# The last product of a decoder block: a gate applied in PSUM, stores queued behind all loads, more rooms, one root for four tiles

## The chip, the cores and the metric

One core of a Trainium2 chip runs the whole kernel. The metric is device time in microseconds (us) of one execution; the number given for a kernel is the median of its runs. Engines: TensorE (PE) multiplies, VectorE (DVE), ScalarE (ACT) and GpSimd (POOL) work on elements, SyncE (SP) issues the DMAs. Each engine serves its instructions in the order in which they stand in its own queue.

## What is computed

The reference is one hybrid decoder block on 1024 tokens of width 1024: sparse attention heads and Mamba-2 heads from one input projection, merged by gates, an output projection, then a SwiGLU feed-forward part and a last norm. Only its end matters here:

```python
h = rms_norm(x, norm2_w[l]) * (1.0 + sc2) + sh2
x = x + gt2 * ((jax.nn.silu(h @ w_gate[l]) * (h @ w_up[l])) @ w_down[l])
return rms_norm(x, norm_f_w)      # x * rsqrt(mean(x^2) + 1e-6) * norm_f_w
```

All is float32. The feed-forward width is 2816, 22 blocks of 128.

## The kernel before

Every float32 product is made of three products of a split operand: a high part (ACT copies it, rounded, into the type float32r) and a low part (DVE or POOL subtracts the high part from the source); `mm3k` (lines 292 to 297) issues high times high, high times low, low times high. The pair of high and low part of a 128x512 block is called a piece.

The down projection (`down`, from line 1975) is a Strassen-Winograd product: seven products instead of eight, in the order P1, P2, P6, P7, P5, P4, P3 (`DOWN`). Each has 11 blocks b of the inner dimension (NB) and four token tiles j, so 44 jobs of three matmuls 128x128x512; the four tiles of a product accumulate in four PSUM banks. For each block two pieces are needed, one of activations (from `actd` in DRAM) and one of `w_down` or of sums of its blocks (`wsd`). `down_load` (line 1938) loads each into a row, a 128x512 staging buffer out of 18 (`row`, lines 1479 to 1489), and lets `part` (line 1712) split it into a room: there are 12 rooms for pieces (`piece`, lines 1491 to 1503), six blocks. For one of the two pieces of a block the low part is made on DVE, for the other on POOL. The loads are asked for six blocks ahead of the block that PE is at (line 2053). For P3 the piece of `w_down` is first multiplied on POOL with gate 2, which lies in `acc[:, 9]` (line 1956).

What a product gives is used in `ends` (from line 1998). After P2, P5 and P4 a half (512 columns) of a tile of the residual x2 is completed: a sum with the bank, a multiplication with gate 2 (`times`, line 1996), the addition to x2 (line 1993); after P3 its bank is only added to x2 (line 2015), because the gate is in the weights already. When a half is complete, `square` (line 2065) lets ACT sum its squares. P2 completes the left halves of the even tiles (t = 0, 2, 4, 6), P5 the right halves of the odd ones, P4 the left halves of the odd ones, P3 the right halves of the even ones. When both halves of a tile are there, `final` (line 2077) takes a root for it (`rsqrt`, lines 249 to 274: three scalings and shifts for the first guess, then three steps of two instructions each) and scales the two halves with the root and the final gain `nf`, and a store of each half to `out` is put into SP's queue (line 2092). For the left halves of the even tiles POOL multiplies with `nf` beforehand (`self.pre`, line 2038) and ACT scales; all others are scaled by DVE in one instruction (L2089).

In P3 the last four blocks are done tile by tile (`LAST = 4`): blocks 0 to 6 for all four tiles, then blocks 7 to 10 for tile j = 0, then for j = 1, and so on. The even tile t is 2j.

The order in each queue is fixed while the program is built, by a small planner (`Flow`, lines 105 to 211). Each step has an engine (A, V, G, D stand for ACT, DVE, POOL and SP's DMAs), a cost in us and a list of what it needs; the planner plays the engines forward with these costs and writes an instruction into its engine's queue when, by that clock, it can start; `first=True` puts a step ahead of the others that are waiting. The chip then runs the queues in that order, at its own speed. DVE's 128x512 operation is planned at 0.6 us times a reserve of 1.15.

Of the kernel before, what the change touches and what calls it, by code (L numbers as in the profile page):

```python
# [11 lines left out]
I32 = mybir.dt.int32  # L12
# [200 lines left out]

class Weights:
# [25 lines left out]
class Kern:  # L240
# [8 lines left out]
    def rsqrt(self, needs, r, n, c, eps, slow=1.0):  # L249
# [16 lines left out]
        e = V(0.07 * slow, needs, lambda: E.tensor_scalar(col(0), col(0), c * 2.0 ** 26, eps * 2.0 ** 26, op0=OP.mult, op1=OP.add))  # L266
        e = V(0.07 * slow, [e], lambda: E.tensor_single_scalar(col(2).bitcast(I32), col(0).bitcast(I32), 1, op=OP.arith_shift_right))

        e = V(0.07 * slow, [e], lambda: E.tensor_scalar(col(2).bitcast(I32), col(2).bitcast(I32), -1, 0x5F3759DF - 2 ** 31,
                                                 op0=OP.mult, op1=OP.add))  # L270
        for f in (3.0, 12.0, 768.0):
            e = V(0.19 * n * slow, [e], products)
            e = V(0.07 * n * slow, [e], lambda f=f: step(f))
# [1217 lines left out]
    def piece(self):  # L1491

        b = Buf(self.rings["pc"], None)

        def make():
            if b.i < 8:
                r, = self.room(self.xroom[b.i])
                return r[:, 0:512], r[:, 512:1024]
            m = b.i - 8
            return tuple(w.t.rearrange("p k c -> p (k c)")[:, 512 * m:512 * m + 512] for w in self.room(*self.wroom))  # L1500

        b.make = make
        return b
# [434 lines left out]
    def down_load(self, p, b):  # L1938
# [5 lines left out]
        for n in range(2):  # L1944
# [9 lines left out]
            if p == 3 and n:  # L1954

                d = G(1.23, [d, self.g2op], lambda x=x: nc.gpsimd.tensor_tensor(x.t, x.t, self.acc[:, 9], op=OP.mult))
# [18 lines left out]
    def down(self):  # L1975
# [14 lines left out]
        LAST = 4  # L1990
# [7 lines left out]
        def ends(p, j, ps, op):  # L1998
# [14 lines left out]
            if p == 3:  # L2013
                t, cs = 2 * j, slice(512, 1024)
                e = V(0.6, [op, ua[j]], lambda: nc.vector.tensor_tensor(x2[:, t, cs], x2[:, t, cs], ps.t, op=OP.add), first=True)
                ps.until(e)
                self.square(t, 1, e)
                self.final(t, nf, nfop)
                return
# [16 lines left out]
            if p == 2:  # L2036

                self.pre[t] = G(1.23, [self.sq[t][0], nfop], lambda: nc.gpsimd.tensor_tensor(xs(), xs(), nf(cs), op=OP.mult))
            if p == 4:
                self.final(t, nf, nfop)  # L2040

        for n, p in enumerate(self.DOWN):
# [3 lines left out]
            for b, j in jobs:  # L2046
# [4 lines left out]
                if j == 0:  # L2051
                    i = n * NB + b
                    while len(self.dl) < min(i + 6, 7 * NB):
                        self.down_more()
                (xp, xe), (wp, we) = self.dl[p, b]
# [9 lines left out]
    def square(self, t, cb, need):  # L2065
# [3 lines left out]
        if t not in self.rf:  # L2069
            self.rf[t] = self.buf("rq" if t % 2 else "rf", [128, 6], f"rq_nf{t}")  # L2070
            self.sq[t] = {}
        r = self.rf[t]
        self.sq[t][cb] = e = A(0.62, [need, jk, r], lambda: nc.scalar.activation(
            jk.t, self.x2[:, t, cs], AF.Square, accum_out=r[:, cb:cb + 1]))
        jk.until(e)

    def final(self, t, nf, nfop):
        nc, x2, sq, r = self.nc, self.x2, self.sq[t], self.rf[t]
# [3 lines left out]
        ends = []  # L2082
        for cb in range(2):
            cs = slice(512 * cb, 512 * cb + 512)
            x = lambda cs=cs: x2[:, t, cs]
            if cb == 0 and t in self.pre:
                w = A(0.61, [self.pre[t], e], lambda x=x: nc.scalar.activation(x(), x(), AF.Copy, scale=r[:, 2:3]))
            else:
                w = V(0.6, [e, nfop], lambda x=x, cs=cs: nc.vector.scalar_tensor_tensor(  # L2089
                    x(), x(), r[:, 2:3], nf(cs), op0=OP.mult, op1=OP.mult))  # L2090
            ends.append(w)
            D(0.73, [w], lambda x=x, cs=cs: nc.sync.dma_start(self.out[t * 128:(t + 1) * 128, cs], x()))
        r.until(*ends)
# [340 lines left out]
```

## Time and profile before

| | us |
|---|---|
| median of 3 runs | 2545.92 (2544.04 to 2547.81) |
| the profiled execution | 2542.33 |
| its span, first to last instruction | 2540.50 |
| PE busy | 2439.7, 96% |
| DVE busy | 1803.7, 71% |
| ACT busy | 1238.7 |
| POOL busy | 1169.3 |
| mean granted clock of TensorE | 0.988 |

The span is what the profiler saw between the first and the last instruction; the execution's own time has 1.83 us more. The page also lists the chain that ended last, waits between engines and the order of time; times in the trace count from the span's start. The down projection begins at 2302.15.

### The profile page before, as it was taken

The numbers are of one execution on the slowest core, as the hardware profiler recorded it, in microseconds if no ns is written. First come the engines' busy times: TensorE is split into PE (matmuls) and PEld (weight loads), VectorE is DVE, ScalarE is ACT, GpSimd is POOL, SyncE is SP. The second block draws the span as 40 slices with busy tenths as digits, with TensorE's granted clock in tenths as the row PEclk, the third lists the DMA queues.
The fourth block names the chain that finished last, engine by engine and source line by source line (L and its number), as shares of the span: only waits on it lengthen the run. The fifth ranks groups of instructions, "written<-read, shape, count | busy, mean of one in ns | idle before, by whom it ended". The sixth has DMA issues, their size and how long they took to land. (4 is left out here: it accounts for less than half of the span.)

```text
span 2540.5 us, 39589 instructions
## 1 busy us (share of the span) xinstructions
PE 2439.7 (96%) x13674; PEld 2082.0 (82%) x13674; DVE 1803.7 (71%) x3937; ACT 1238.7 (49%) x2640; POOL 1169.3 (46%) x931
## 2 busy tenths in 40 slices
PE   5999999999999999999999899999989999999996
PEld 5999878889889888988877677878978888888885
DVE  7644787876766687765467786778787676664769
ACT  4421667666656566655555455532452332324443
POOL 2112474735465646464533341201355565555655
PEclk8999999999999999999999899999999999999998
DMA  7433443323335423233355675427323232337753
GB/s 249 131 124 98 141 120 92 108 80 100 92 100 173 141 95 114 80 101 97 122 173 184 224 234 186 157 65 253 125 72 112 91 112 93 103 121 283 226 159 112
DMA packets 265161, 345.55 MB, mean 136 GB/s; under 512 B 21112, under 2 KB 177528, under 8 KB 264448
## 3 DMA queue, kind: packets, MB, share of 16 engines
q1 hardware_dynamic: 264960, 343.02, 42.1%
q8 instruction: 108, 1.77, 0.3%
q14 instruction: 93, 0.76, 0.1%
HBM read 247.13 MB, written 95.81 MB: 135 GB/s over the span
## 5 line engine op out<-in xcount | busy, mean ns | idle before, releaser
L2190 POOL TENSOR_SCALAR P<-P,sm,gate 128x640 f32<-128x640 f32 (+7 forms) x256 | 215.2, 851 | 247.1 <-DVE sm L2187 186.6
L2261 DVE TENSOR_TENSOR kv<-tp,kv 128x512 fp32r<-128x512 f32 (+1 forms) x296 | 189.8, 657 | 108.1 <-ACT kv L2260 106.9
L2260 ACT ACTIVATE kv<-tp 128x512 fp32r<-128x512 f32 (+1 forms) x296 | 165.1, 574 | 184.0 <-PE tp L2257 176.6
L2181 ACT ACTIVATE P<-P,sm 128x640 f32<-128x640 f32 (+7 forms) x256 | 187.5, 734 | 45.9 <-DVE sm L2177 43.7
L1070 PE MATMUL o<-kv 128*128 128x512 f32 x528 | 189.6, 411 | 12.4 <-DVE kv L2261 8.8
L2172 PE MATMUL S<-kv,Q 128*128 128x384 f32 (+5 forms) x768 | 182.6, 336 | 3.0 <-DVE sm L2177 3.0
L2177 DVE CUSTOM_DVE_ANT_0 P<-S,kb 128x256 f32<-128x256 f32 (+5 forms) x256 | 120.5, 495 | 56.7 <-PE tp L2257 29.5
L1137 DVE SCALAR_TENSOR_TENSOR u<-xr,hcw,u 128x512 f32<-128x512 f32 x144 | 150.2, 1043 | 13.3 <-ACT u L1140 8.3
L295 PE MATMUL fps<-hT_hi,whi_x 128*128 128x512 f32 x384 | 157.3, 410 | 0.1
L1717 ACT ACTIVATE x1r<-ex 128x512 fp32r<-128x512 f32 x147 | 89.7, 627 | 135.4 <-POOL ex L1736 31.2
L1851 DVE TENSOR_TENSOR ex<-ex,gu 128x512 f32<-128x512 f32 x122 | 82.1, 684 | 99.1 <-PE gu L297 98.1
L2257 PE MATMUL tp<-id,P 128*128 128x128 f32 x1056 | 151.8, 272 | 0.5 <-POOL P L2190 0.5
L297 PE MATMUL fps<-hT_hi,wlo_x 128*128 128x512 f32 x384 | 151.0, 393 | 0.0
L296 PE MATMUL fps<-hT_lo,whi_x 128*128 128x512 f32 x384 | 151.0, 393 | 0.0
L295 PE MATMUL fps<-whi_z,hT_hi 128*128 128x256 f32 x512 | 149.8, 293 | 0.1
L1719 DVE TENSOR_TENSOR x1r<-ex,x1r 128x512 fp32r<-128x512 f32 x102 | 122.6, 1213 | 33.3 <-ACT x1r L1717 33.0
L2257 PEld LDWEIGHTS tp<-id,P 128*128 128x128 f32 x1056 | 127.2, 140 | 21.1 <-POOL P L2190 0.8
L297 PE MATMUL fps<-whi_z,hT_lo 128*128 128x256 f32 x512 | 144.4, 282 | 0.0
L296 PE MATMUL fps<-wlo_z,hT_hi 128*128 128x256 f32 x512 | 144.3, 282 | 0.0
L2172 PEld LDWEIGHTS S<-kv,Q 128*128 128x128 f32 x768 | 128.2, 189 | 17.9 <-DVE sm L2177 2.4
L1070 PEld LDWEIGHTS o<-kv 128*128 128x128 f32 x528 | 95.7, 189 | 34.6 <-DVE kv L2261 16.7
L2331 POOL TENSOR_TENSOR dx<-xs,hd 128x512 f32<-128x512 f32 x32 | 43.4, 1355 | 170.2 <-DVE yy L2373 127.9
(443 smaller groups left out, 8022.3 us busy)
## 6 DMA issues: line engine op xcount, KB each, us to landing
wada<-w_ada SPq DMA_DIRECT2D x40, 512.0 KB, 4.2
ex<-actd SPq DMA_DIRECT2D x73, 256.0 KB, 3.1
actd<-ex SPq DMA_DIRECT2D x69, 256.0 KB, 2.0
ac<-acd SPq DMA_DIRECT2D x32, 512.0 KB, 5.0
raw_x<-w_in SPq DMA_DIRECT2D x24, 512.0 KB, 4.4
ws<-w_down SPq DMA_DIRECT2D x44, 256.0 KB, 3.6
wsd<-ws SPq DMA_DIRECT2D x88, 128.0 KB, 1.8
ff<-w_gate SPq DMA_DIRECT2D x22, 512.0 KB, 5.0
```

The lines of the kernel that those rows point to most:

```text
L295: mm(ps, lh, rh, start=k == 0, stop=False)
L296: mm(ps, lh, rl, start=False, stop=False)
L297: mm(ps, ll, rh, start=False, stop=k == kt - 1)
L1070: nc.tensor.matmul(o.t.rearrange("p h q -> p (h q)"), vst(), pair()[m], start=n + m == 0, stop=n == u.total - 1 and m == 1)
L1137: nc.vector.scalar_tensor_tensor(u.t, xr[:, k:k + N2], hcw[:, ft, k:k + 1], u.t, op0=OP.mult, op1=OP.add)
L1719: return E(cost, [x], lambda: eng.tensor_tensor(k4(p.t[1]), src(), k4(p.t[0]), op=OP.subtract), first=first)
L2172: mm(sp[:, :w], q, kvb.kv[:, br, r, first + c0:first + c1], start=r == 0, stop=r == 1)
L2181: ex = A(0.26 + 0.8333e-3 * n, [mx], lambda: nc.scalar.activation(P[:, :n], P[:, :n], AF.Exp, bias=sm[:, 1, h:h + 1], scale=-1.0, accum_ou ...
L2190: nc.gpsimd.tensor_scalar(P[:, :n], P[:, :n], sm[:, 3, m:m + 1], k.gate[:, i, self.h0 + m, br + 1:br + 2], op0=OP.mult, op1=OP.mult)
L2257: nc.tensor.transpose(tp[:, h * 128:h * 128 + 128], P, k.id)
L2260: hi = A(0.064 + 0.104 * n, [op, pair], lambda: nc.scalar.activation(pair()[0][:, c], tp[:, c], AF.Copy))
L2261: lo = V(0.068 + 0.133 * n, [hi], lambda: nc.vector.tensor_sub(pair()[1][:, c], tp[:, c], pair()[0][:, c]))
```

## The change

- Gate 2 is no longer multiplied into the pieces of `w_down` for P3 on POOL. Instead, each bank of P3 is multiplied with it in PSUM on DVE, ahead of the addition to x2.
- P3's last six blocks, not four, are done tile by tile.
- There are 20 rooms for pieces: eight more in M1, the low parts of the feed-forward's input, free after the last gate/up product. The loads are asked for nine blocks ahead, not six.
- The four odd tiles get one root together after P4. Their sums of squares lie in `acc[:, 12]`; the root works on 128x4 operands, so a step is three instructions (two multiplications for the products, one for the step) for all four tiles. Even tiles keep a root each.
- The right halves of the odd tiles, completed by P5, are multiplied with `nf` on POOL beforehand and scaled on ACT; their left halves are scaled by DVE.
- The stores of the odd tiles are queued after the last load has been asked for, and need it (`self.dlast`). The stores of the even tiles are queued as before.

```diff
+class Roots:
+    def __getitem__(self, key):
+        return self.buf[:, 12, key[1]]
...
+        if n > 2:
+            def products():
+                y, t = col(n), col(2 * n)
+                E.tensor_tensor(t, y, y, op=OP.mult)
+                E.tensor_tensor(t, t, col(0), op=OP.mult)
+            def step(f):
+                y, t = col(n), col(2 * n)
+                E.scalar_tensor_tensor(y, t, -f, y, op0=OP.add, op1=OP.mult)
...
+            if b.i > 11:
+                return tuple(self.M1[:, (b.i - 12) // 2, 2 * ((b.i - 12) % 2) + r] for r in range(2))
...
-            if p == 3 and n:
-                d = G(1.23, [d, self.g2op], lambda x=x: nc.gpsimd.tensor_tensor(x.t, x.t, self.acc[:, 9], op=OP.mult))
+            self.dlast = d
...
-        LAST = 4
+        LAST = 6
+        self.rings["pc"] += [[self.ffend] for _ in range(8)]
+        outs, root = [], lambda m, n=4: acc[:, 12, m:m + n]
...
             if p == 3:
                 t, cs = 2 * j, slice(512, 1024)
-                e = V(0.6, [op, ua[j]], lambda: nc.vector.tensor_tensor(x2[:, t, cs], x2[:, t, cs], ps.t, op=OP.add), first=True)
+                e = V(0.6, [op], lambda: nc.vector.tensor_tensor(ps.t, ps.t, acc[:, 9], op=OP.mult), first=True)
+                e = V(0.6, [e, ua[j]], lambda: nc.vector.tensor_tensor(x2[:, t, cs], x2[:, t, cs], ps.t, op=OP.add), first=True)
...
-            if p == 2:
-                self.pre[t] = G(1.23, [self.sq[t][0], nfop], lambda: nc.gpsimd.tensor_tensor(xs(), xs(), nf(cs), op=OP.mult))
-            if p == 4:
-                self.final(t, nf, nfop)
+            if p in (2, 5):
+                self.pre[t] = G(1.23, [self.sq[t][c], nfop], lambda: nc.gpsimd.tensor_tensor(xs(), xs(), nf(cs), op=OP.mult))
+            if p == 4 and j == 3:
+                sq = [self.sq[t][c] for t in (1, 3, 5, 7) for c in range(2)]
+                e = V(0.07, sq, lambda: nc.vector.tensor_tensor(root(0), root(0), root(12), op=OP.add))
+                e = self.rsqrt([e], Roots(acc), 4, 1.0 / 1024, EPS)
+                for t in (1, 3, 5, 7):
+                    outs.extend(self.scaled(t, 1, e, lambda t=t: acc[:, 12, 4 + t // 2:5 + t // 2], nf, nfop))
+        AHEAD = 9
...
-                    while len(self.dl) < min(i + 6, 7 * NB):
+                    while len(self.dl) < min(i + AHEAD, 7 * NB):
                         self.down_more()
+                    if not self.dnext:
+                        for t, cb, w in outs:
+                            self.store(t, cb, [w, self.dlast])
+                        outs.clear()
```

## Rows read from the trace of the kernel before

**Rows 1.** Busy us by stretch; length, PE, PEld, DVE, ACT, POOL, clock, DMA share, GB/s.

```profile
2302.15:2332.76 30.61, 30.61 (x133) 24.80 (x132) 13.02 (x13) 9.98 (x16) 17.63 (x12) 1.00 0.92 328
2332.76:2364.18 31.42, 30.93 (x133) 24.74 (x132) 21.42 (x16) 17.49 (x31) 21.44 (x14) 1.00 0.86 308
...
2456.22:2486.89 30.67, 30.67 (x134) 24.78 (x133) 30.67 (x31) 11.75 (x25) 19.41 (x12) 1.00 0.43 129
2486.89:2517.60 30.71, 21.96 (x91) 16.41 (x89) 29.62 (x56) 11.47 (x25) 22.72 (x15) 0.92 0.31 100
2517.60:2531.30 13.70, 12.06 (x42) 8.94 (x42) 12.56 (x39) 3.81 (x9) 2.76 (x2) 0.80 0.32 121
2531.30:2540.50 9.20, 0.00 (x0) 0.00 (x0) 5.30 (x24) 2.79 (x5) 0.00 (x0) 0.62 0.46 172
```

**Rows 2.** Waits of PE from 2302 to 2541: waiter, releaser, us, times, longest.

```profile
PE dps L295 <- ACT x1r L1717: 6.8, 1, 6.8
PE dps L296 <- DVE x1r L1719: 2.2, 3, 1.3
PE dps L296 <- POOL x1r L1719: 1.4, 1, 1.4
PE dps L296 <- POOL wlo_pc L1719: 0.5, 1, 0.5
```

**Rows 3.** Order of time, PE; start, length, instruction, [idle before, releaser].

```profile
2510.74 0.39 PE L297 MATMUL dps<-x1r,wlo_pc 128*128 128x512 f32 x1
2517.92 0.80 PE L295 MATMUL dps<-x1r,x1r 128*128 128x512 f32 x1 [6.80 <-ACT x1r L1717]
...
2521.04 0.63 PE L295 MATMUL dps<-x1r,whi_pc 128*128 128x512 f32 x1
2521.47 0.63 PE L296 MATMUL dps<-x1r,whi_pc 128*128 128x512 f32 x1
```

**Rows 4.** Order of time, SP's queue.

```profile
2491.44 0.33 SPq L1953 DMA_DIRECT2D ex<-w_down  x1
2512.28 1.00 SPq L2092 DMA_DIRECT2D out<-x  x2
...
2513.84 0.46 SPq L1953 DMA_DIRECT2D ex<-w_down  x1
```

**Rows 5.** Order of time, DVE.

```profile
2478.12 0.67 DVE L1993 TENSOR_TENSOR ex<-acc,dps 128x512 f32<-128x512 f32 x1
...
2481.90 1.78 DVE L1719 TENSOR_TENSOR x1r<-ex,x1r 128x512 fp32r<-128x512 f32 x1
...
2485.30 0.68 DVE L1993 TENSOR_TENSOR x<-x,ex 128x512 f32<-128x512 f32 x1
2485.90 0.68 DVE L1993 TENSOR_TENSOR x<-x,acc 128x512 f32<-128x512 f32 x1
...
2488.86 0.85 DVE L1719 TENSOR_TENSOR wlo_pc<-ex,whi_pc 128x512 fp32r<-128x512 f32 x1 [0.87 <-ACT whi_pc L1717]
...
2511.52 1.40 DVE L2089 SCALAR_TENSOR_TENSOR x<-x,rq_nf,acc 128x512 f32<-128x512 f32 x2
...
2519.29 0.68 DVE L1719 TENSOR_TENSOR x1r<-ex,x1r 128x512 fp32r<-128x512 f32 x1
```

**Rows 6.** POOL's gate multiplications by line: count, ns min/median/max, first and last start.

```profile
L1956 POOL TENSOR_TENSOR ex<-ex,acc x10: 1278/1742/1826, 2474.2 to 2517.3; 128x512 f32<-128x512 f32 x10
```

**Rows 7.** Order of time, DVE: one root by itself, and what follows.

```profile
2521.57 0.14 DVE L266 TENSOR_SCALAR rq_nf<-rq_nf 128x1 f32<-128x1 f32 x1
...
2523.52 0.68 DVE L2015 TENSOR_TENSOR x<-x,dps 128x512 f32<-128x512 f32 x1
```

**Rows 8.** Order of time, DVE: behind PE's end.

```profile
2531.32 0.69 DVE L2015 TENSOR_TENSOR x<-x,dps 128x512 f32<-128x512 f32 x1 [0.60 <-PE dps L297]
...
2532.86 0.16 DVE L2080 TENSOR_TENSOR rq_nf<-rq_nf 128x1 f32<-128x1 f32 x1
...
2535.95 0.75 DVE L2089 SCALAR_TENSOR_TENSOR x<-x,rq_nf,acc 128x512 f32<-128x512 f32 x1
```

## What I expect of the change, and why

> **What bounds the kernel now.** I read the busy time of each engine by stretch first, one stretch for each of the seven products of the down projection [rows 1]. TensorE (PE) is the bound of the whole kernel, so the question is only where it is not fed. A product of 44 jobs takes 30.67 us when nothing holds it, 0.697 us a job; the second product, P6, takes 31.42 us. The last one, P3, runs from 2486.89 to 2531.30, that is 44.41 us. So PE loses 13.74 us in the last product and 0.75 us in P6, and nothing in the other five (P1, 30.61, and P4, 30.67, stand for them). Behind PE's end lie 9.20 us more.
>
> The waits of PE name the loss [rows 2], and the order of time shows it [rows 3]: one wait of 6.8 us and some small ones; after the long one the granted clock of the stretch is 0.80 [rows 1], and matmuls that follow each other start 0.43 us apart instead of 0.233 (0.697 / 3).
>
> The wait ends on ScalarE (ACT), which makes the high part of a piece, but ACT is not the cause. SyncE's (SP's) queue is [rows 4]: the load of block 9 is issued at 2491.44, the next entry is a store of `out` that starts at 2512.28, and only behind it come the loads of block 10, the last at 2513.84; PE goes on at 2517.92, 4.1 us after that. The store waited for VectorE (DVE): the scaling of tile 1 (L2089) starts at 2511.52 [rows 5]. The hand-made plan put the store ahead of the loads because it thought DVE faster than it is.
>
> Why is DVE late? It is busy for 30.67 of 30.67 us in the sixth product and for 29.62 of 30.71 us in the stretch behind it [rows 1]. Its `tensor_tensor` on 128x512 with one operand in PSUM takes 0.67 us; with both in SBUF it takes 0.68 us or 1.78 us, and starts 0.60 us apart where nothing is in the way [rows 5]. GpSimd (POOL) is the cause of the 1.78, since it runs its own 128x512 operations then: it is busy 19.41 and 22.72 us in those two stretches. So a DVE operation that meets one of POOL's pays some 1.10 us.
>
> A page of the Trainium skill states this as a rule: SBUF — State Buffer, section "Who interferes with whom", says that a VectorE instruction with two SBUF inputs and a GpSimd instruction that reads SBUF block each other fully, whereas with one SBUF input there is no conflict. The rows agree in kind, with 1.10 us for a collision. The rule also speaks against one step of the change, the four new POOL products of the sixth stage: they fall where DVE has no idle time. If each blocked a DVE operation for its own shortest time, 1.28 us [rows 6], that would be an estimated 5.1 us of DVE against 4.4 us by the rows; both are outweighed by what is taken off POOL, and the sum below doesn't use the rule.
>
> **Part by part.**
>
> *Gate in PSUM.* POOL loses eleven multiplications of w_down pieces (ten in one row, 1.74 us in the median) [rows 6], some 18 us in the last two stages; it gains four products with the final gain (one for each odd tile), by the same kind of row about 6 us. If each meets one DVE operation, DVE gets back 7 x 1.10 = 7.7 us. DVE gains four products in PSUM at 0.60 us each; three lie beside PE's work, the fourth is behind the last matmul: +0.6 us at the end.
>
> *Stores behind all loads.* The 13.74 us are this step's to take: the loads of block 10 no longer stand behind a store. With nine blocks ahead they can be queued when the last product is at block 2, 2486.89 + 8 x 0.697 = 2492.5, instead of 2513. The sixteen stores themselves need no room of their own: the DMA share is 0.31 and 0.32 in these stretches [rows 1]. What is queued behind the waiting stores on SP is now only other stores, and no engine waits for those.
>
> *More rooms, nine ahead instead of six.* Three blocks are 8.4 us more of PE time between a load and its use. P6's 0.75 us went when the load of x2 (4 MB) filled the DMAs (share 0.92 and 0.86 [rows 1]); nine blocks are 25 us of cover. I take all of it back, with 0 and 0.75 as ends. The extra loads come in the stretch with 0.92: 3 x 0.5 MB at its 328 GB/s is 4.8 us, under the 16.7 us that six blocks covered already, so I cost it at nothing; without that cover it would be up to 4.8 us.
>
> *Last six blocks tile by tile.* Each even tile's end then comes 6 x 0.697 = 4.18 us after the one before instead of 2.79, so DVE can finish one before the next. The price: block 10 is needed by job 26 of 44, at 2486.89 + 25 x 0.697 = 2504.3, instead of job 32, 4.2 us later.
>
> Does DVE make that? From 2488.86 on it has eight low parts to do before (first and last in [rows 5]); with three blocks more lead five. In front of the last one stand also the twelve steps of the fifth result block (P4). That makes 17 x 0.60 = 10.2 us, and POOL still has five low parts, 5 x 1.10 = 5.5 us of blocking: 2488.9 + 15.7 = 2504.6. So PE would wait 0.3 us. The lower bound is 0. The upper: the lead doesn't come about (the 18 rows of staging, not the pieces, limit it), then 20 x 0.60 + 8 x 1.10 = 20.8 us, 2509.7, and a wait of 5.4 us; a wait like this costs clock too, ten matmuls at 0.43 instead of 0.233, 2.0 us.
>
> *One root for four tiles.* A root is ten small DVE instructions; alone, from the first scaling to what comes behind takes 1.95 us [rows 7], and 0.2 us more for the addition ahead. Four roots for the odd tiles become one of 13 instructions, about 2.6 us at the same 0.2 us each. Four of the eight odd scalings go to ACT, which has 11.47 us of work in 30.71. DVE saves up to 4 x 2.15 - 2.6 = 6.0 us, less where the roots were interleaved, and 4 x 0.66 = 2.6 us of scaling. It is off PE's path; it matters for the tail.
>
> *The tail.* Now the last addition starts at 2531.32, its root at 2532.86, the last scaling at 2535.95, the span ends at 2540.50 [rows 8]. Between 2532.86 and 2535.95 the roots of tiles 4 and 6 are interleaved: 3.09 us against 2.15 alone. With 4.18 us between tiles tile 4 should be nearly through, so -0.95 us, and +0.6 us for the product in PSUM. But DVE may come late: after 2504.6 it has the odd root and four scalings (2.6 + 2.6), till 2509.8, while the first even tile is there at 2505; each even tile costs it 0.60 + 0.60 + 2.15 + 0.66 = 4.0 us if its root runs alone, some 3.0 if interleaved. Three of them end at 2518.8 to 2521.8 where PE ends at 2517.6 + 0.3. So 0.9 to 3.9 us late; by the planner's habit of interleaving I take 1.5. Tail together: +0.6 - 0.95 + 1.5 = +1.15 us.
>
> **Sum.** 13.74 + 0.75 - 0.3 - 1.15 = 13.0 us. The profiled execution took 2542.33 us, its span 2540.50, 1.83 us around it; it becomes 2529.3. The median of the three runs, 2545.92, lies 3.6 us over the profiled one, and the new runs should scatter like the old: 2545.9 - 13.0 = **2532.9 us**. A difference under 0.2%, 5.1 us, can't be told from none.
>
> **Rivals.**
> 1. DVE is still the bound, in the place of the store (the lead doesn't come, or the squares on ACT, which wait for DVE, hold the high parts of the last pieces). For it: DVE without idle time in two stretches; ACT is served in order. Against: fewer POOL operations, and the lows are put first. Price: wait 5.4 and clock 2.0, tail lateness then 1.5: 13.74 + 0.75 - 7.4 - 1.15 = 5.9 us gained, 2540.0. Half of it, 2.7 + 1.0, gives 9.6, 2536.3.
> 2. Slower: a load of block 10 takes a staging row that a late DVE step of P4 or a square frees, and SP waits in order, with everything behind. From the moment X at which block 10 is split, 19 jobs remain: 13.2 us, clock 2.0, tail 9.2 - 0.35. The old end is reached at X = 2516.4; the kernel is slower from there on, 12 us after the piece is needed, and by more than 0.2% from X = 2521.6. DVE would have to be as late as in the kernel before with 8 to 14 us less to do. Price at X = 2524: +7.6 us, 2553.5.
> 3. It doesn't do what it says: the plan still has a store ahead of a load. For the odd tiles the need of the last load excludes it; the first even store comes after job 26, which itself needs the last load. It would give about today's time, 2546.
> 4. The first stage, DMA-bound, pays the 4.8 us: gain 8, 2538.
>
> **How the numbers follow.** Forecast (gain 11 to 15) 0.55; rival 1 in its half and full form 0.27; rival 4 0.05; rival 2 0.08, half of it slower by over 0.2%; rival 3 0.05, within 0.2%, or a little slower. Faster by over 0.2%: 0.55 + 0.23 of rival 1 + 0.05 = 0.83; slower 0.05; within 0.2% 0.12. The range: at best no wait and no lateness, 13.74 + 0.75 + 0.35 = 14.8, and the runs' scatter of 1.9 us: 2529.3. Above it takes in rival 1 in full with some scatter, 2541.5.
>
> **What would show it.** SP: all loads before the first store of `out`. PE: no wait over 1 us in the last product, which takes 31 to 32 us at clock 1.00; P6 at 30.7. POOL: no multiplication ahead of a low part. DVE: five or six low parts behind the start of the last product, one chain of root steps on 128x4 operands. Tail 10 to 10.7 us. The forecast is wrong if PE waits over 3 us for DVE, ACT or a load before job 26, or if the tail grows by more than 4 us.

## The result, and the profile after

| | before | after |
|---|---|---|
| median, us | 2545.9 (2542.68 to 2547.81, 6 runs) | 2531.89 (2528.1 to 2536.19, 6 runs) |
| the profiled execution, us | 2542.33 | 2536.19 |
| its span | 2540.50 | 2534.4 |
| ratio to before | | 0.9947 [0.9938, 0.9957] |

The change gains 14.0 us in the medians; 13.0 were forecast. Its profiled execution is its slowest run, and spent 7.17 us more on the code in front of the down projection, which the change leaves as it is: the down projection began at 2309.32 instead of 2302.15. In the profiles below that start lies anywhere from 2301.3 to 2312.9. So I compare stage lengths, each taken from the start of the first matmul of a product to that of the next, and call the stretch from the first matmul of the down projection to the end of the span "down". Down is 238.35 us before and 225.08 after, 13.27 less.

The busy time by stretch of the kernel after, to be read like [rows 1]; the stretches are the first product, the second (P2, which the prediction calls P6), the sixth (P4), the last (P3) and what is behind PE's end:

```profile
2309.32:2341.21 31.89, 30.77 (x134) 24.71 (x132) 19.47 (x16) 14.09 (x24) 24.05 (x15) 1.00 0.69 239
2341.21:2371.63 30.42, 30.42 (x133) 24.81 (x132) 18.64 (x13) 19.02 (x32) 19.46 (x12) 1.00 1.01 375
2462.68:2493.12 30.44, 30.44 (x134) 24.79 (x133) 28.87 (x32) 12.85 (x28) 18.36 (x12) 1.00 0.45 138
2493.12:2523.85 30.73, 30.73 (x133) 24.59 (x131) 28.01 (x63) 11.89 (x28) 8.93 (x6) 1.00 0.23 87
2523.85:2534.40 10.55, 0.00 (x0) 0.00 (x0) 6.48 (x25) 2.85 (x5) 0.00 (x0) 0.67 0.40 150
```

The last product has no wait left: PE is busy for all of its 30.73 us, at a granted clock of 1.00. DVE's share is hardly lower, 28.01 us of 30.73 where its first 30.71 us had 29.62; POOL has 8.93 us of work in the whole product where it had 25.48 (22.72 and 2.76 in [rows 1]).

SP's queue at the end, where [rows 4] has a store between the loads:

```profile
2489.79 0.32 SPq L1982 DMA_DIRECT2D ex<-actd  x1
2490.60 0.33 SPq L1982 DMA_DIRECT2D ex<-w_down  x1
2512.45 19.18 SPq L2147 DMA_DIRECT2D out<-x  x16
```

The last two loads go out 2.5 us before the last product begins, and all sixteen stores stand behind them.

DVE in the order of time, to be read like [rows 5] and [rows 8]: the last low part of a piece (L1748), the one root for the odd tiles (first and last instruction), the odd scalings, then for tile 6 the product in PSUM and the last scaling:

```profile
2506.34 0.68 DVE L1748 TENSOR_TENSOR M<-ex,M 128x512 fp32r<-128x512 f32 x1
...
2509.09 0.16 DVE L2073 TENSOR_TENSOR acc<-acc 128x4 f32<-128x4 f32 x1 [0.86 <-ACT ex L2116]
...
2511.47 0.16 DVE L284 SCALAR_TENSOR_TENSOR acc<-acc 128x4 f32<-128x4 f32 x1
2511.67 2.08 DVE L2140 SCALAR_TENSOR_TENSOR x<-x,acc 128x512 f32<-128x512 f32 x3
...
2524.92 0.69 DVE L2045 TENSOR_TENSOR dps<-dps,acc 128x512 f32<-128x512 f32 x1
...
2530.04 0.75 DVE L2140 SCALAR_TENSOR_TENSOR x<-x,rq_nf,acc 128x512 f32<-128x512 f32 x1
```

The last low part ends 13.9 us into the last product and is needed 17.3 us into it. In [rows 5] the last one stood at 2519.29, 32.4 us into the product. The product in PSUM starts 1.07 us after PE's end.

The one wait of PE over 0.6 us is new and lies in the first product. PE and POOL, in the order of time:

```profile
2312.55 8.52 POOL L1748 TENSOR_TENSOR M<-ex,M 128x512 fp32r<-128x512 f32 x5
...
2319.43 0.50 PE L324 MATMUL dps<-M 128*128 128x512 f32 x1 [1.12 <-POOL M L1748]
```

Five low parts that go into the new rooms (M) stand in a row on POOL, and PE waits for one of them.

The difference by stage: last product 13.67 us less, second 1.00 less, the four in the middle 1.22 less together (30.34 to 30.44 instead of 30.67 to 30.70), first 1.28 more, tail 1.34 more. That makes 13.27.

Most of the second product's part comes and goes from trace to trace. The wait of 0.49 us for a low part on POOL that made it 31.42 us ([rows 2], its last line) is there in two of the seven traces of kernels that run six blocks ahead: before, and shorter in e_four_order (31.15). In the other five (e_stores, e_gate, e_gatestores, e_lead6, e_rootslate) the product takes 30.67 us without any change to it. So 0.75 us of the 13.27, and of nearly every difference to before in the table below, can't be credited to the change.

### The profile page after: what moved, and what is told of

Read it like the earlier page. It is cut to its first block, busy times and chain, and to the rows that moved or that the text cites. A ratio compares the mean times of both kernels' runs of the same rounds, so it can differ in the third digit from the quotient of the medians.

```text
span 2534.4 us, 39552 instructions
## 1 busy us (share of the span) xinstructions
PE 2439.8 (96%) x13674; PEld 2086.5 (82%) x13674; DVE 1793.8 (71%) x3910; ACT 1238.3 (49%) x2644; POOL 1163.2 (46%) x924
## 4 chain that ended last, share of the span: by engine, by line
PE 79%; DVE 11%; DMA 5%; issue 2%; ACT 2%; POOL 1%; SPq 0%; ACTq 0%; DVEq 0%; POOLq 0%
PE fps L322 7%; PE fps L324 7%; PE fps L323 7%; PE gu L322 5%; PE gu L324 5%; PE gu L323 5%; PE o L1097 4%; PE S L2226 4%; PE tp L2311 4%; DVE u L1164 3%; PE dps L323 2%; PE dps L324 2%; PE dps L322 2%; PE sps L322 2%; PE sps L324 2%
## 5 line engine op out<-in xcount | busy, mean ns | idle before, releaser
L2231 DVE CUSTOM_DVE_ANT_0 P<-S,kb 128x256 f32<-128x256 f32 (+5 forms) x256 | 120.3, 494 | 56.5 <-PE tp L2311 30.2
L1746 ACT ACTIVATE x1r<-ex 128x512 fp32r<-128x512 f32 x115 | 70.5, 626 | 104.6 <-POOL ex L1765 31.1
L1748 DVE TENSOR_TENSOR x1r<-ex,x1r 128x512 fp32r<-128x512 f32 x89 | 107.9, 1223 | 14.1 <-ACT x1r L1746 13.8
```

What stands on the lines that cost most here:

```text
L2231: nc.vector.tensor_tensor_reduce(P[:, c0:c1], sp[:, :w], k.kb[:, m0:m0 + w], scale=-1.0, scalar=sm[:, 0, h:h + 1] if p else 3.0e38, op0=OP ...
```

## The experiments

The prediction puts the lost 13.7 us down to one thing, a store that stands ahead of block 10's loads on SP. Its rival is that the last low parts are late by themselves, on POOL and DVE. This table holds all kernels; times are us, worked out as above, each from one trace. The last product ends with PE's last matmul; the tail is what is left from there to the end of the span.

| kernel | first product | last product | tail | down |
|---|---|---|---|---|
| before | 30.61 | 44.40 | 9.21 | 238.35 |
| e_stores: before, odd stores behind all loads | 30.62 | 44.34 | 9.08 | 237.40 |
| e_gate: before, gate in PSUM | 30.61 | 32.61 | 12.16 | 228.75 |
| e_lead: before, nine ahead | 31.90 | 33.73 | 16.39 | 233.93 |
| e_gatelead: before, both of these | 31.99 | 30.67 | 10.67 | 225.24 |
| e_gatestores: before, gate in PSUM, odd stores behind | 30.61 | 30.89 | 14.01 | 228.88 |
| after | 31.89 | 30.73 | 10.55 | 225.08 |
| e_gatepool: after, gate on POOL | 31.94 | 47.59 | 8.13 | 239.57 |
| e_lead6: after, six ahead | 30.61 | 40.66 | 9.56 | 234.20 |
| e_four_order: e_lead6, four roots, odd stores not deferred | 30.62 | 41.28 | 9.48 | 235.22 |
| e_rootslate: e_lead6, odd root behind the last low parts | 30.62 | 36.38 | 9.57 | 229.94 |
| e_both: after, late rooms, odd halves all on ACT | 30.41 | 30.68 | 14.01 | 227.20 |
| e_nowroom: after, four rooms closed | 31.54 | 31.14 | 13.57 | 225.85 |
| e_best: after, late rooms, four closed, more in PSUM | 30.41 | 30.08 | 9.51 | 219.60 |

### The order of the stores alone

```diff
-            D(0.73, [w], lambda x=x, cs=cs: nc.sync.dma_start(self.out[t * 128:(t + 1) * 128, cs], x()))
+            if t % 2:
+                self.outs.append((x, t, cs, w))
...
+                    if not self.dnext:
+                        for x, t, cs, w in self.outs:
+                            D(0.73, [w, self.dlast], lambda x=x, t=t, cs=cs: nc.sync.dma_start(self.out[t * 128:(t + 1) * 128, cs], x()))
...
```

> The kernel before with one edit: the stores of the odd tiles are queued behind the last load and need it. Gate on POOL, 12 rooms, six blocks ahead, four roots and LAST = 4 stay. Lengths from the trace: down projection (first matmul of P1 to the end of the span) 238.35 us before, 225.08 after; last product 44.41 and 30.73. Theory (the order in SP's queue cost the time): the wait of 6.8 us goes, last product 33 to 36, down projection 228 to 231, since POOL with its eleven multiplications still holds the last pieces a little. Rival (DVE and POOL were the bound and the store only stood there): last product over 39, down projection over 233. If the edit alone does everything: last product under 32.

Measured: 2544.1 us, ratio 0.9993 [0.9984, 1.0003]: no change. The last product takes 44.34 us and down 237.40, over the rival's 39 and 233; the theory's 33 to 36 failed. In the order of time, SP, DVE, ACT and PE:

```profile
2492.70 0.32 SPq L1953 DMA_DIRECT2D ex<-actd  x1
2493.25 0.33 SPq L1953 DMA_DIRECT2D ex<-w_down  x1
2511.78 4.01 SPq L2058 DMA_DIRECT2D out<-x  x4
...
2514.04 1.40 DVE L2094 SCALAR_TENSOR_TENSOR x<-x,rq_nf,acc 128x512 f32<-128x512 f32 x2
...
2516.20 0.63 ACT L2078 ACTIVATE sl<-x 128x512 f32<-128x512 f32 x1 [5.56 <-DVE x L1994]
...
2516.22 0.67 DVE L1719 TENSOR_TENSOR x1r<-ex,x1r 128x512 fp32r<-128x512 f32 x1
...
2516.94 0.79 PE L296 MATMUL dps<-x1r,x1r 128*128 128x512 f32 x1 [5.46 <-DVE x1r L1719]
```

The loads of block 10 now go out at 2492.70 and 2493.25, some 20 us earlier than in [rows 4], and it doesn't help. The low part of block 10 stands in DVE's queue behind scalings of odd tiles, and one of its high parts stands in ACT's queue behind a square that waits 5.56 us for DVE. PE's long wait is still there, 5.46 us, and ends on DVE. The store was one of two things that were late at the same time.

### Undoing one part of the change at a time

For e_lead6 (six ahead, 12 rooms):

```diff
-        self.rings["pc"] += [[self.ffend] for _ in range(8)]
...
-        AHEAD = 9
+        AHEAD = 6
```

> The changed kernel with 12 rooms and six blocks ahead again; the gate in PSUM, the late stores, one root and LAST = 6 stay. Theory (order in SP's queue, the rooms are not needed for it): last product 31 to 33; P1 back to 30.6 (31.89 after), P6 back to 31.4 (30.42), the products between 30.67 instead of 30.35 since no piece lies in M1; down projection 225.5 to 228. Rival (the deeper lead is what feeds the last product): last product over 35, down projection over 230.

> The changed kernel with three of its parts undone: 12 rooms and six ahead, a root for each odd tile, stores of the odd tiles queued as before; so two stores of an odd tile stand ahead of the last two loads again. The gate in PSUM and LAST = 6 stay. Theory (order): PE waits for the last block, 5 us or more, last product 36 to 42, in spite of POOL's lighter load. Rival (POOL's multiplications made DVE late, without them the stores are early enough): no wait over 2 us, last product under 33.

For e_gatepool:

```diff
+            if p == 3 and n:
+                d = G(1.23, [d, self.g2op], lambda x=x: nc.gpsimd.tensor_tensor(x.t, x.t, self.acc[:, 9], op=OP.mult))
...
-                e = V(0.6, [op], lambda: nc.vector.tensor_tensor(ps.t, ps.t, acc[:, 9], op=OP.mult), first=True)
...
```

> The changed kernel with the gate multiplied into the pieces of w_down on POOL again, not in PSUM; all else as changed. POOL gets eleven operations of some 1.7 us back, DVE loses four products of 0.6 us. Theory (order): last product 30.5 to 32.5, tail (10.55 us after) 9.5 to 11, down projection 224.5 to 227. Rival (POOL's load was the cause): PE waits for low parts, last product over 34.

Measured, one execution each: e_lead6 2538.15 us, e_four_order 2549.95, e_gatepool 2546.8, beside 2545.64 for the kernel before. In e_lead6 and e_gatepool the theory (order in SP's queue) failed and the rival held: last products of 40.66 and 47.59 us, where under 33 was expected. e_four_order's 41.28 lies in the expected 36 to 42, but it says little for the order of the stores, since e_lead6 with its stores behind the loads is at 40.66. The second product of e_lead6 didn't go back to the expected 31.4 us; it stayed at 30.67. By the table, putting the gate back on POOL costs 14.49 us of down, which is more than the whole gain, and going back to six ahead costs 9.12. Going back to four roots and the planner's order of stores on top of that (e_four_order against e_lead6) costs 1.02, 0.48 of it in the second product. e_four_order has its two last loads behind two stores again, at 2516.48 and 2516.91, where e_lead6 issues them at 2493.19 and 2493.79; the last product is only 0.62 us longer for it. Its start, 2312.88 against 2302.20, is most of what makes it 11.8 us slower in the single time.

### Adding one part at a time to the kernel before

e_gate has the change's two lines for P3 in `ends` and drops POOL's multiplication; e_lead has the M1 rooms and 9 for 6; e_gatelead has both. All keep four odd roots, `LAST = 4` and the store lines of before.

> The kernel before with gate 2 applied in PSUM by VectorE (two additions of the change's edit to the last product) and nothing else: POOL's ten gate multiplications are gone, the pieces still come six blocks ahead, the order by job is as before (last four blocks tile by tile). Of the kernel before: last product 44.40 us, from the first matmul of the last chain of products to the end 238.35 us. Theory (POOL's multiplications hold up its own low parts and stretch VectorE's): POOL is busy under 12 us in the last product instead of 22.7 and the last product takes 34 to 42 us, the second product keeps its 31.4 and the first its 30.6. Rival (the order of VectorE's queue alone, which this does not touch: the last low part still stands behind the four odd roots): 43 to 45 us.

> The kernel before with the pieces nine blocks ahead instead of six, the eight new rooms in the freed act tiles, and nothing else: POOL still applies gate 2 ten times, four odd roots, last four blocks tile by tile. Theory (both the multiplications and the place of the last low parts in VectorE's queue count): last product 36 to 44 us, from 44.40; the first product 31.9 instead of 30.6, the middle ones 30.35 instead of 30.67. Rival (POOL's work alone counts): 43.5 to 48 us, as the multiplications then fall closer together.

> The kernel before with both of these, the gate in PSUM and the pieces nine blocks ahead, but with its four odd roots, its order of stores and its last four blocks tile by tile. Theory (the two are nearly the whole gain, and the one root and the order of six tile by tile add little to it): last product 30.5 to 32 us, the chain of products to the end 225 to 228 us, 0.995 to 0.996 of the kernel before. Rival (the change needs its one root and the deferred stores as well): last product 34 us or more, 0.997 or more.

Measured: e_gate 2539.36 us and e_lead 2545.14 (one execution each, before 2544.25), e_gatelead 2534.04 us, ratio 0.9957 [0.994, 0.9974]. The last products of e_gate and e_lead, 32.61 and 33.73 us, are shorter than expected (34 to 42 and 36 to 44); e_gatelead lies in all of its ranges. The gate alone takes 9.60 us off down, the lead alone 4.42, both 13.11; after has 13.27. (The lead's 4.42 don't show in its single time, since its down projection began at 2309.47.) So these two parts are the whole gain, and the one root, the six blocks tile by tile, POOL's products with `nf` and the deferred stores together add 0.16 us of down, nothing that can be told from none. In the last product each of the two takes off more than 10 us by itself; what the lead alone leaves is in its tail, 16.39 us. There POOL still does its multiplications (it is busy for 18.43 us of that product, DVE for 30.93 of 33.73), and DVE is late: its last addition of a bank starts 7.3 us behind PE's end.

Why does the one root gain nothing? From the sixth product on, DVE's small instructions add up to 9.73 us in after and 14.88 in e_gatelead, and its scalings to 6.00 and 8.95. But DVE is busy nearly as long, 63.36 us (28.87, 28.01 and 6.48 in the rows above) for 63.73. POOL has 5.65 us more to do in after, about its four products with `nf`, and DVE's steps on two operands in SBUF got longer, for instance seven of the multiplications with gate 2 for P5 and P4, first in e_gatelead, then in after:

```profile
L1996 DVE TENSOR_TENSOR ex<-ex,acc 128x512 f32<-128x512 f32 x7 | 6.9, 994 | 0.0
L2026 DVE TENSOR_TENSOR ex<-ex,acc 128x512 f32<-128x512 f32 x7 | 9.9, 1441 | 0.0
```

That POOL's four products stretch them fits the rows, but wasn't tried alone.

One pair of the table shows what the rest of the change costs without the lead. e_four_order and e_gate both run six ahead, with the gate in PSUM, four odd roots and the planner's order of stores. e_four_order has, besides, the six blocks tile by tile and POOL's four products with `nf` (with the scalings on ACT that go with them). Its last product takes 41.28 us for 32.61, and its down is 6.47 us longer. So part of the 9.12 us that the lead is worth in after is a cost of these two parts that the lead covers. Which of the two it is wasn't tried.

What holds e_gate up now? SP and PE in the order of time:

```profile
2509.34 1.00 SPq L2090 DMA_DIRECT2D out<-x  x2
2510.43 0.41 SPq L1953 DMA_DIRECT2D ex<-actd  x1
2510.89 0.45 SPq L1953 DMA_DIRECT2D ex<-w_down  x1
...
2514.95 0.50 PE L295 MATMUL dps<-x1r,x1r 128*128 128x512 f32 x1 [0.32 <-ACT x1r L1717]
2516.34 0.51 PE L296 MATMUL dps<-x1r,x1r 128*128 128x512 f32 x1 [0.89 <-POOL x1r L1719]
```

Here the store is late alone: the loads behind it land just too late, and PE waits 0.32 and 0.89 us. Its price can be had by taking it away too:

> The kernel before with the gate in PSUM (as in e_gate) and, as well, the odd tiles' stores queued behind the loads of the last two blocks (as in e_stores); pieces six ahead, four odd roots, last four blocks tile by tile. In e_gate two stores stood on SP at 2509.34 ahead of the loads of block 10 (2510.43 and 2510.89), whose high part ran at 2513.72, and the last product took 32.61 us with the tail 12.16. Theory (with the gate off POOL the order of the stores becomes the next bound, which it was not while POOL held the gate): last product 30.6 to 31.4 us, chain of products to the end 225 to 227 us, as much as the whole change, and without its 1.28 us in the first product. Rival (VectorE's queue alone sets the last low parts, and the stores cost nothing here either): 32.3 to 33 us and 228 to 229 us.

Measured: 2534.82 us, ratio 0.9954 [0.994, 0.9969]. The last product falls to 30.89, as the theory had it, but down stays: 228.88 against 228.75. In SP's queue and on DVE:

```profile
2497.37 0.33 SPq L1953 DMA_DIRECT2D ex<-w_down  x1
2509.93 10.40 SPq L2056 DMA_DIRECT2D out<-x  x8
...
2526.63 0.69 DVE L2013 TENSOR_TENSOR dps<-dps,acc 128x512 f32<-128x512 f32 x1
```

PE ends at 2523.19 and DVE takes the last bank at 2526.63, 3.4 us later: it is the bound, and PE's 1.7 us only came out as a longer tail. So the expected 225 to 227 us of down failed, and the store's order is worth nothing in either kernel in which I took it alone.

### Place in the queue, or amount of work?

e_rootslate is e_lead6 with the same instructions, but the odd root also needs the low parts of block 10, which puts it behind them in DVE's queue:

```diff
-                e = V(0.07, sq, lambda: nc.vector.tensor_tensor(root(0), root(0), root(12), op=OP.add))
...
+                late.extend(sq)
...
+                    if not self.dnext and late:
+                        e = V(0.07, late + [x for _, y in self.dl[3, 10] for x in (y if isinstance(y, (list, tuple)) else [y])], lambda: nc.vector.tensor_tensor(root(0), root(0), root(12), op=OP.add))
...
```

> The changed kernel with its pieces six blocks ahead, as in e_lead6 (last product 40.66 us, the last low part on VectorE at 2510.94 behind the one odd root and three odd scalings), but the odd root now also waits for the low parts of block 10, so that in VectorE's queue it stands behind them and not ahead of them. The work is the same. Theory (the place in the queue is what delays the last low parts): the last low part ends 5 to 7 us earlier and the last product takes 33 to 36 us. Rival (the amount of VectorE's work in that stretch, not its order): 39 to 41.5 us.

Measured: 2536.05 us in one execution, last product 36.38 us. DVE in the order of time, e_lead6 first:

```profile
2503.75 0.16 DVE L2072 TENSOR_TENSOR acc<-acc 128x4 f32<-128x4 f32 x1 [0.25 <-ACT ex L2115]
...
2507.87 3.14 DVE L2139 SCALAR_TENSOR_TENSOR x<-x,acc 128x512 f32<-128x512 f32 x3
2510.94 0.68 DVE L1748 TENSOR_TENSOR x1r<-ex,x1r 128x512 fp32r<-128x512 f32 x1
```

Then e_rootslate:

```profile
2507.89 0.89 DVE L1748 TENSOR_TENSOR x1r<-ex,x1r 128x512 fp32r<-128x512 f32 x1 [0.87 <-ACT x1r L1746]
2508.70 1.22 DVE L2089 TENSOR_TENSOR acc<-acc 128x4 f32<-128x4 f32 x1
```

DVE's last low part starts 24.8 us into the last product in the first and 19.6 in the second, 5.1 us earlier and inside the expected 5 to 7, and the product is 4.28 us shorter with the same work. At 36.38 us it is just over the 33 to 36 us that I expected, and far from the rival's 39 to 41.5. The place in the queue is worth 4.3 of the 10 us by which e_lead6's last product is over 30.67. In what is left of it PE still waits four times, 0.68 to 0.93 us each, for DVE, ACT and POOL, at a mean granted clock of 0.95; these waits weren't taken apart further.

### What the first product and the rooms cost, and a better kernel

After loses 1.28 us in the first product, and its tail has DVE 1.07 us late. e_both takes both on: the new rooms and the nine blocks only from block 3 of the first product on, and POOL multiplies the odd left halves with `nf` too, so that ACT scales all eight odd halves.

```diff
+                if (n, b, j) == (0, 3, 0):
+                    self.rings["pc"] += [[self.ffend] for _ in range(8)]
+                    AHEAD = 9
...
-            if p in (2, 5):
+            if p != 7:
```

> The changed kernel with two edits: it runs six blocks ahead and uses no room of the freed act tiles until block 3 of the first product, then nine; and POOL multiplies the left halves of the odd tiles by the final norm's weight beforehand too, so that ScalarE scales both halves of the odd tiles and VectorE has four scalings (2.74 us) fewer. Theory (the 1.28 us lost in the first product come from pieces that wait for rooms of the act tiles and from five low parts in a row on POOL; VectorE's lateness of 1.07 us at the sixth tile comes from the odd root and scalings): first product 30.4 to 30.7 us instead of 31.89, tail 9.3 to 10 us instead of 10.55, chain of products to the end 222.8 to 223.8 us instead of 225.08. Rival (the first product's loss is there whatever the rooms, as nine blocks have to be loaded and split at some time): loss moves to a later product, 224.5 to 225.5 us.

Measured: 2532.24 us, ratio 0.9943 [0.9926, 0.9959]. The first product takes 30.41 us and the later ones keep their length, as expected. The second edit went wrong; ACT and DVE in the order of time:

```profile
2506.46 5.02 ACT L2140 ACTIVATE x<-x,acc 128x512 f32<-128x512 f32 x8 [4.31 <-DVE acc L284]
...
2512.13 0.16 DVE L2125 TENSOR_TENSOR rq_nf<-rq_nf 128x1 f32<-128x1 f32 x1 [4.42 <-ACT ex L2118]
```

Eight scalings in a row on ACT stand ahead of tile 0's square, so tile 0's root, and with it everything behind it in DVE's queue, waits 4.42 us. The tail is 14.01 us, so the expected 222.8 to 223.8 us of down became 227.20. The bound moved from DVE to a queue that I had filled.

The products two to six of after take some 30.35 us (30.34 to 30.44) where those of before that have no wait take 30.67 to 30.70, which I hadn't foreseen. In after, PE, a run of matmuls from the new rooms and one with an operand in the room named whi_pc:

```profile
2419.88 0.39 PE L322 MATMUL dps<-M 128*128 128x512 f32 x1
2420.10 0.39 PE L323 MATMUL dps<-M 128*128 128x512 f32 x1
2420.33 0.39 PE L324 MATMUL dps<-M 128*128 128x512 f32 x1
...
2422.64 0.39 PE L322 MATMUL dps<-x1r,whi_pc 128*128 128x512 f32 x1
2422.88 0.40 PE L323 MATMUL dps<-x1r,whi_pc 128*128 128x512 f32 x1
2423.11 0.39 PE L324 MATMUL dps<-x1r,wlo_pc 128*128 128x512 f32 x1
```

In the unbroken runs of each kind around these, they start 0.2267 us (2419.65 to 2421.01, six steps) and 0.2336 us (2421.24 to 2423.81, eleven steps) apart; the 0.2285 us of the expectation below is a mean over stretches in which the two kinds border on each other. e_nowroom is after without the four rooms in whi and wlo, eight blocks ahead:

```diff
+        self.rings["pc"].shut = True
+        for n in range(8, 12):
+            self.rings["pc"][n] = None
...
-        AHEAD = 9
+        AHEAD = 8
```

> The changed kernel, its pieces kept out of the four rooms named whi_pc and wlo_pc in all seven products, so that all lie in rooms named x1r or M; eight blocks ahead, since four rooms are gone. Nothing else differs. In the changed kernel matmuls with an operand in whi_pc or wlo_pc followed each other at 0.234 us and the others at 0.2285 us, and a product took 30.35 us. Theory (it is the room that matters): every matmul at 0.2285 us, products without stalls 30.15 to 30.2 us. Rival (it is the mix or the size of the working set): 30.3 us or more.

Measured: 2530.91 us in one execution. Products two to six take 29.92 us each, 0.2267 a matmul, less than the expected 30.15 to 30.2 and far from the rival's 30.3 or more: it is the room. (It isn't the size of the working set either: before, with only 12 rooms, takes 30.67.) But down is 225.85, with a wait for DVE in the last product (31.14) and a tail of 13.57. PE gained, and DVE was not ready for it.

So DVE is what is left, and the next kernel tests whether its operations are stretched where they work beside POOL. e_best combines the late rooms and the closed ones with one new edit: P2, P5 and P4 add and gate in PSUM as well.

```diff
-            e = plus([op, u[j], y], yt, src, pt)
...
+                e = plus([f], pt, src, pt)
...
+                e = plus([op, u[j]], pt, src, pt)
...
-            e = times([e], yt, yt, c)
-            e = plus([e, x2op[j // 2]], xs, xs, yt)
-            y.until(e)
+            e = times([e], pt, pt, c)
+            e = plus([e, x2op[j // 2]], xs, xs, pt)
+            ps.until(e)
```

> The changed kernel with three edits. First, pieces run six blocks ahead until block 3 of the first product and eight after it, and the rooms of the act tiles are used only from there (as in e_both). Second, from there no piece lies in the rooms named whi_pc and wlo_pc (as in e_nowroom). Third, new: the second, fifth and sixth product in order of running (the ones numbered 2, 5 and 4 in the code) add their partial sum and apply their gate in PSUM too, so that VectorE's addition and gate there no longer read two operands from SBUF, and no row is needed for them; VectorE's count of instructions is the same. Theory (VectorE's 128x512 operations take 1.78 us instead of 0.68 only where both operands lie in SBUF while POOL works, and VectorE's lateness in the last product is what made the tail 13.6 to 14.0 us in e_both and e_nowroom): first product 30.0 to 30.5 us, the five after it 29.92 each, last product 29.9 to 30.1, tail 9 to 10 us, chain of products to the end 218.5 to 220.5 us (225.08 in the changed kernel), 0.991 to 0.993 of the kernel before. Rival (POOL stretches VectorE's operations wherever the operands lie): VectorE as late as in e_nowroom, last product 30.5 to 31.2, tail 12 to 13.6, 223 to 224.5 us and 0.9935 to 0.995.

Measured: **2524.53 us** (2523.81 to 2529.26, 5 runs), ratio 0.9923 [0.991, 0.9937]; the interval of after is [0.9938, 0.9957]. Every length came as the theory had it. The first two edits had run before, in e_both and e_nowroom; the third wasn't run alone. Its stretches (first product, sixth, last, tail):

```profile
2302.40:2332.81 30.41, 30.41 (x133) 24.79 (x132) 17.19 (x15) 13.62 (x22) 22.17 (x14) 1.00 0.96 343
2452.49:2482.41 29.92, 29.92 (x133) 24.77 (x132) 28.01 (x36) 15.25 (x30) 23.08 (x15) 1.00 0.46 150
2482.41:2512.49 30.08, 30.08 (x133) 24.59 (x131) 25.23 (x65) 13.26 (x28) 5.21 (x5) 1.00 0.24 88
2512.49:2522.00 9.51, 0.00 (x1) 0.00 (x0) 5.49 (x20) 2.17 (x4) 0.00 (x0) 0.70 0.44 165
```

And DVE's groups of the steps of P4 and P5 in the sixth and last product, by line and shape (busy us, mean ns, idle before), before:

```profile
L1993 DVE TENSOR_TENSOR x<-x,ex 128x512 f32<-128x512 f32 x8 | 9.1, 1138 | 0.0
L1996 DVE TENSOR_TENSOR ex<-ex,acc 128x512 f32<-128x512 f32 x8 | 8.1, 1017 | 0.0
```

and in e_best:

```profile
L2033 DVE TENSOR_TENSOR dps<-dps,acc 128x512 f32<-128x512 f32 x8 | 5.5, 685 | 0.0
L2030 DVE TENSOR_TENSOR x<-x,dps 128x512 f32<-128x512 f32 x8 | 5.4, 676 | 0.0
L2030 DVE TENSOR_TENSOR x<-x,acc 128x512 f32<-128x512 f32 x4 | 3.8, 956 | 0.0
```

The same sums and products take 676 to 685 ns with an operand in PSUM and 1017 to 1138 with both in SBUF. In the same kernel and stretch the four with both in SBUF (last line) still take 956. The Trainium skill, page SBUF — State Buffer, section "Who interferes with whom", states the rule behind it: a VectorE instruction contends with GpSimd's reads when it has two SBUF inputs, and not when it has at most one and is in none of the modes that use both ports. These groups agree, with 0.28 us (956 to 676) a piece on the mean.

## Why the prediction was right, and where it was wrong

The time was right, 2531.89 for 2532.9, and so was the reading of what PE lost in the last product, 13.74 us. What gave it back was named wrongly. That the sum held all the same was luck: it took in nearly all that PE could regain, whichever step regained it. The signs that the prediction named couldn't tell either. All loads stood ahead of the stores, PE had no wait, and the tail was 10.55 us (the last product, 30.73 us, and DVE's three low parts behind its start came in under the 31 to 32 us and the five or six), and all of this is there, too, when the gate and the lead do the work.

- **Stores behind all loads.** "The 13.74 us are this step's to take": this is the step that failed. Taken alone it gives nothing (e_stores), and beside the gate in PSUM nothing either (e_gatestores). I followed the chain from PE's wait to ACT, to the load, to the store, and stopped at the first cause that explained it all. The rows already had the second one: DVE without a pause [rows 1], and its last low part at 2519.29 [rows 5]. Rival 1 of the prediction, DVE in the place of the store, was the true bound of the kernel before, not a danger after it. Its sign, DVE without idle time, was right.
- **Gate in PSUM.** Costed at 7.7 us of DVE and no PE time; it is the largest part, 9.60 us of down alone and 14.49 when undone. The price on DVE was about right. From the sixth product to the end DVE is busy for 69.51 us in e_gate and 78.15 in [rows 1], though it has four products of 0.69 us more: 11.4 us for eleven multiplications, 1.04 each, where the prediction has 1.10. What was missing is that PE waits for this time. POOL has 17.6 us less in the last two products of after (27.29 for 44.89), where 18 less and 6 more were forecast; four of its low parts come earlier. The 0.6 us that it adds to the end can't be told apart from the rest of the tail.
- **Nine ahead.** Costed at 0.75 us in the second product and as cover elsewhere. It is the other part of the gain: 4.42 us alone, 9.12 when undone. In part that is so because it moves the last low parts ahead of the odd root and the scalings in DVE's queue (4.3 us by e_rootslate); the rest is not shown step by step. The second product's wait is gone, but five of seven traces with six ahead don't have it, so 0.75 us was no price of six ahead. The sentence "I cost it at nothing" was wrong by 1.28 us, in the first product, as rival 4 had it but by another way: not DMA (its share fell to 0.69) but five low parts in a row on POOL, for rooms that come free only as the product starts. e_both, in which that is put off, has 30.41 us there.
- **When the loads go out.** 2492.5, 5.6 us into the last product, was the planner's clock. The chip issued them 2.5 us before that product. The planner fixes the order only.
- **Six blocks tile by tile.** The low part was to be ready 17.7 us into the product and PE to wait 0.3; it was ready at 13.9, and PE didn't wait. The upper bound, a wait of 5.4 us and 2.0 of clock if the lead fails, was the right kind of danger: e_lead6, with six ahead, loses 10 us in its last product, e_gate, with six ahead and four blocks tile by tile, 1.9. With the gate on POOL and nine ahead it is the same: e_gatepool's down is 5.64 us longer than e_lead's. (Both pairs differ in the roots and the order of stores too; `LAST` was not tried alone.) The nearest pair, e_four_order and e_gate, gives 6.47 us of down for six tile by tile together with POOL's four products. Against that, after's tail is 0.12 us shorter than e_gatelead's.
- **One root.** Predicted 2.6 us long, measured 2.58 (2509.09 to 2511.67). Its saving on DVE came out near the forecast, step by step, but the sum of DVE's busy time is hardly lower than in e_gatelead (63.36 for 63.73 us), and the tail of e_gatelead, with four roots, is the same. The prediction had weighed POOL's four products against what is taken off POOL; beside e_gatelead, where that is gone already, they are what stands against the root.
- **Tail.** +1.15 forecast, +1.34 measured; DVE 1.07 us late at tile 6 for 1.5.
- **Not in the sum.** The four middle products gained 1.22 us by the rooms, about what the first one lost.

So the sum came out by two terms that were worth more than I had for them, in the place of one that was worth nothing.

## What to carry to other kernels

When an operand is late, list every queue that its steps stand in and ask of each when it would have been done had the others been on time; the first late link of a chain hides those that are late beside it. Take the cheapest suspect away alone before you credit it, and judge by the stretch up to the end of the kernel: three times here (e_lead, e_gatestores, e_nowroom) PE's gain came back in part or whole as a longer tail, since DVE was the bound. Where VectorE works beside GpSimd, an operand left in PSUM can be cheaper than the same operand in SBUF (0.676 for 0.956 us here).

## What the runs showed of the hardware

- Matmuls of the same shape followed each other at 0.2267 us with their pieces in the rooms x1r and M, and at 0.2336 us with one in whi_pc or wlo_pc. A product of 132 took 29.92 us without those rooms, 30.35 in after, 30.67 before. Which property of the rooms does it was not tried.
- Small DVE instructions can be held up beside POOL too: the first instruction of the odd root in e_rootslate, on 128x4, took 1.22 us (2508.70 to 2509.92, as long as a 128x512 operation of POOL went on, 2508.18 to 2509.91) where the same instruction takes 0.16 in after and e_lead6. What stands behind that was not tried either.
